# One written order for TensorE in an expert stage, with a split gather, late sums and fewer keep-warm products

## The chip, the cores and the metric

The kernel runs on one NeuronCore of a Trainium2 chip. The metric is the device time of one execution in microseconds. A profile of one execution shows where it goes. Engines are PE (TensorE; PEld is its weight load), DVE (VectorE), ACT (ScalarE), POOL (GpSimd) and SP, which here only issues DMAs.

## The reference

The network is two blocks on 256 tokens of width 1024, all in float32. The first is attention (eight differential half-heads and eight block-attention heads) followed by a mixture of 32 experts; the second is a state-space layer, a stick-breaking attention and two gated embeddings. The change touches the experts. What they compute, with `t` the normed tokens:

```
g = argmax(t @ router_group); top two of the group's eight experts, weights p_group * softmax(top two)
for each expert e and each token sent to it:
    hid = silu(t @ w_gate[e]) * (t @ w_up[e])        # 1024 -> 256
    y[token] += weight * (hid @ w_down[e])           # 256 -> 1024
x = x + y
```

## The kernel before, in words

**Weights.** Each weight is read once. A `Ring` (L89) loads tiles of 1 MB (128 x 2048 floats) from SP's queue in the order of use into the free slots of several pools. A slot comes free when the reads of its tile are through. The 32 experts are 96 such tiles: eight groups of four experts, and per group eight tiles for gate and up (`k` = 0 to 7) and four for down (two halves of columns `c`, two row blocks `k`). Two more tiles, for the embeddings of the second block, are taken behind the third and the fifth group. The tiles of the state-space layer may go into four of the slots alone.

**A group `g` of four experts.** Each expert has 32 slots for tokens, so a group has 128.
- `dispatch` (DVE) writes `disp[g]`, the one-hot of token against slot. There is one buffer for it.
- `gather`: the inputs of the slots, transposed, are products of `x` with `disp[g]`: eight blocks of 128, in two halves `j`. A half is eight matmuls into the one PSUM bank `gx`. Four operations then move it to the tile `xg` with the gain, by turns on DVE (L928) and ACT (L926).
- `pv`: 32 matmuls (eight tiles, four experts beside each other in the array's columns) into one bank; `slot_scale` gives each slot the factor of its token (`rs`); ACT's silu and a DVE operation make `sl`.
- `combine_T` transposes the weighted one-hot: `cmb` says which slot goes to which token, `sw` is the slot's weight.
- Two transposes of `sl` and a DVE copy (L1015) give `hT`. The down products follow: per half `c` eight matmuls into a bank, which ACT moves to `oe` (L1027), times `sw`.
- Two matmuls of `oe` with `cmb` add the half into `sums_of[t][c]`, which stay in PSUM through all groups. Behind the last group they are added to `x`.

**What sets the order.** A planner puts the operations of each engine into an order ahead of time, from their dependencies, from when it thinks that operands are there, and from the order in the program. `after(late, early)` gives it an extra edge, and `in_turn` (L964) chains products: each behind the one before it. Before the change the pv and down products of all groups are in this chain, and the transposes and the sums of the last group. The gather, `slot_scale`, `combine_T`, the other transposes and sums and the projections `ple_proj` are not: the planner places them where it likes. In the trace they stand between the chained products at changing places.

**Other parts of the stage.** `ple_proj` (behind groups 2 and 4, counted from 0) multiplies half of the embedding's input by one weight tile: four units of two matmuls, each into `gx`, each moved out by ACT (L957). Behind group 1 stands `overflow`, a branch for tokens that have no slot; here it isn't taken, but no product crosses it. `keep_warm` (L299) issues products that nobody reads; `warm(7, j)` puts `TAIL[j]` of them between the products of the last group: `j` = 0 to 3 behind tiles k = 3 to 6 of pv, 4 ahead of the transposes, 5 to 8 behind the four down tiles, 9 at the end.

Of the kernel before, what the change touches and what calls it, by code (L numbers as in the profile page):

```python
# [9 lines left out]
F = mybir.dt.float32  # L10
# [10 lines left out]
P = 128  # L21
# [7 lines left out]
# columns of the small-parameter pack  # L29
# [9 lines left out]
# columns of the constant packs  # L39
# [21 lines left out]
TAIL = (8, 3, 3, 2, 1, 3, 2, 3, 2, 6)  # L61
# [3 lines left out]
def merge(*parts):  # L65
    """Runs generators side by side, each at the pace of its number of steps."""
    live = [[g, n, 0] for g, n in parts]
    while live:
        live.sort(key=lambda a: a[2] / a[1])
        a = live[0]  # L70
        a[2] += 1
        try:
            next(a[0])
        except StopIteration:
            live.remove(a)
# [13 lines left out]
class Ring:  # L89
    """Weight tiles of 1 MB in the order of use, loaded ahead into the free slots of a few pools."""  # L90
# [6 lines left out]
    def add(self, name, pool, slots, bufs=None, once=False):  # L97
        """Slots of a tag of a pool, for use again and again or once."""
# [24 lines left out]
    def issue(self):  # L123
        """All reads of the oldest tile taken are in the program."""
# [7 lines left out]
class Halves:  # L132
    """Two tiles [128, 4, 2, 256] as one of [128, 8, 2, 256]."""
# [11 lines left out]
class Dense:  # L145
    """Splits weight tiles into two parts of twelve bits each, ahead of their products."""
# [55 lines left out]
def tile_network(ctx, tc, A, out, dbg=None):  # L202
# [14 lines left out]
    def mm(o, lhsT, rhs, **kw):  # L217
        """A product, issued behind the earlier ones into the same bank."""
# [32 lines left out]
    # ---------------------------------------------------------------- loads that come first  # L251
# [47 lines left out]
    def keep_warm(n, behind, bank=None):  # L299
        """Products that nobody reads: the tensor engine's clock stays up while it waits for data."""  # L300
# [17 lines left out]
    def row_scale(tok, junk, behind):  # L318
        """1 / root mean square of each token."""
# [41 lines left out]
    def scale_of(t, r, sums, eps=EPS):  # L361
        """1 / root of the sum of the two halves' squares."""
# [8 lines left out]
    def tick():  # L371
        """Half a weight tile has been multiplied: emits what was put off until now."""
# [38 lines left out]
    def trans(dense, xT, evac):  # L411
        """out[512 columns, token], K = 1024, weights standing; evac gets two blocks of 128 columns."""
# [50 lines left out]
    # ================================================================ first block: attention  # L463
# [45 lines left out]
    def products(q, k, blk, both):  # L509
        """The products of two heads, side by side in the upper and the lower half of the array."""  # L510
# [7 lines left out]
    def softmax(pa, b):  # L518
        """Exponentials of the masked scores of one head less their maximum, and 1 / their sums."""
# [16 lines left out]
    def transposed(w):  # L536
        """[128 queries, 384] -> [128 keys, 384]: keys 0.. for all queries, keys 128.. for the later ones."""
# [21 lines left out]
    def forward(b, acc):  # L559
        """The parts of block b of yT, and acc with its queries in their order."""  # L560
# [73 lines left out]
    # bias of a distance, as a Hankel table through DRAM: queries run backwards within their tiles of 128  # L634
# [15 lines left out]
    # -lambda on all partitions  # L650
# [325 lines left out]
    def next_xg(g):  # L976
        """The inputs of the four experts after those of g."""
        if g == 7:
            return xg
# [628 lines left out]
```

## Time and profile before

| | |
|---|---|
| three runs, us | 773.49, 777.23, 777.46 (median 777.23) |
| span of the profiled execution, us | 773.4 (the page has no other time of it) |
| busy: PE, PEld | 734.3 us (95%), 517.3 us (67%) |
| busy: DVE, ACT, POOL | 60%, 49%, 14% |
| DMA | 188.77 MB, mean 244 GB/s |

Busy shares are means over the whole span. A matmul's row in the trace lasts until its modelled end, and the next may start long before that: a matmul of four beside each other has a row of about 0.6 us, and four of them start within a few nanoseconds. So a busy PE isn't a full one, and the distance from start to start is the better measure. In this kernel one float32 matmul leaves two records, so `x8` in a row of the timeline is four matmuls. "idle before <- X" says how long the engine had been without work and what released it. `gx`, `tp`, `pv` and `acc` are PSUM banks; `w` are weight tiles.

### The profile page before, as it was taken

Reading aid. Unit: us, or ns where it says so; the run is one execution under the profiler, and the core shown is the slowest. Engines: PE = TensorE matmul, PEld = TensorE weight load, DVE = VectorE, ACT = ScalarE, POOL = GpSimd, SP = SyncE. Lnnn points to the kernel's source line nnn. Section 1 sums busy time; section 2 is a strip of 40 time slices with the busy share of each in tenths; the row PEclk is TensorE's granted clock in tenths of the full one; section 3 lists DMA queues with packets and bytes.
Section 4 is the critical chain, followed back from the end, with each engine's and each line's share of the span. In section 5 each row is a group of like instructions: output and inputs, shape, how many; then the busy total and the mean of one; then the engine's idle time right before and its main releaser. Section 6 shows DMA issues by size and latency. Waiting matters only on the chain. (4 is left out here: it accounts for less than half of the span.)

```text
span 773.4 us, 11374 instructions
## 1 busy us (share of the span) xinstructions
PE 734.3 (95%) x4386; PEld 517.3 (67%) x4386; DVE 467.0 (60%) x887; ACT 380.1 (49%) x712; POOL 110.2 (14%) x74
## 2 busy tenths in 40 slices
PE   8999999997899998899999989999899999999997
PEld 5777767542534334333999988897688897766686
DVE  5658675411101102104999979899888656888974
ACT  6557654210121111103776848475577645756763
POOL 0302300000000000000022231413300301242100
PEclk9999999999899999999999999999999999999999
DMA  8994767899999999983466445444354455222211
GB/s 334 423 404 147 264 238 264 308 412 422 413 422 418 421 420 420 422 369 108 165 242 227 160 151 194 175 164 163 110 184 163 164 177 205 72 104 100 107 56 55
DMA packets 29878, 188.77 MB, mean 244 GB/s; under 512 B 3215, under 2 KB 5852, under 8 KB 8188
## 3 DMA queue, kind: packets, MB, share of 16 engines
q1 hardware_dynamic: 29164, 186.70, 62.5%
q8 instruction: 36, 0.59, 0.3%
q10 hardware_dynamic: 416, 0.62, 0.3%
q0 software_dynamic: 240, 0.67, 0.2%
q14 instruction: 22, 0.18, 0.1%
HBM read 186.88 MB, written 1.10 MB: 243 GB/s over the span
## 5 line engine op out<-in xcount | busy, mean ns | idle before, releaser
L183 DVE TENSOR_TENSOR wl<-w,wh 128x1024 fp32r<-128x1024 f32 x116 | 150.4, 1301 | 49.8 <-ACT wh L172 49.6
L172 ACT ACTIVATE wh<-w 128x1024 fp32r<-128x1024 f32 x117 | 123.1, 1057 | 100.2 <-PE dn L219 86.0
L219 PE MATMUL dn<-uC,wh 128*128 128x256 f32 x640 | 119.5, 288 | 0.6 <-ACT uC L346 0.3
L219 PEld LDWEIGHTS dn<-uC,wh 128*128 128x128 f32 x640 | 100.5, 193 | 2.5 <-issue 1.6
L219 PE MATMUL dn<-uC,wl 128*128 128x256 f32 x320 | 91.2, 285 | 0.0
L187 POOL TENSOR_TENSOR wl<-w,wh 128x1024 fp32r<-128x1024 f32 x18 | 46.6, 2587 | 146.2 <-DVE wh L176 98.4
L997 PE MATMUL pv<-w,xg 128*32 128x512 f32 x512 | 65.8, 596 | 0.0
L219 PEld LDWEIGHTS dn<-uC,wl 128*128 128x128 f32 x320 | 61.9, 193 | 0.2 <-issue 0.2
L315 POOL TENSOR_TENSOR rs_r<-rs_v,mhalf 128x8 f32<-128x8 f32 (+2 forms) x26 | 42.7, 1643 | 119.7 <-DVE rs_v L313 103.5
L928 DVE TENSOR_SCALAR xg<-gx,idg 128x128 f32<-128x128 f32 x30 | 10.5, 350 | 72.0 <-PE gx L219 54.0
L219 PEld LDWEIGHTS gx<-disp,x 128*128 128x128 f32 x240 | 31.1, 200 | 23.6 <-issue 15.3
L219 PE MATMUL dn<-wh,uk 128*128 128x512 f32 x128 | 44.5, 406 | 0.0
L219 PE MATMUL dn<-wh,yTg 128*128 128x512 f32 x128 | 44.2, 407 | 0.3
L219 PE MATMUL gx<-disp,x 128*128 128x128 f32 x240 | 36.2, 296 | 7.7 <-PEq L845 5.0
L936 DVE COPY rs<-tp 128x1 f32<-128x1 f32 x8 | 1.3, 159 | 68.2 <-PE tp L219 68.2
L997 PEld LDWEIGHTS pv<-w,xg 128*32 128x32 f32 x512 | 16.1, 109 | 37.6 <-issue 34.4
L1021 PE MATMUL tp<-w,hT 128*32 128x512 f32 x256 | 37.3, 627 | 1.3 <-DVE hT L1015 1.3
L219 PE MATMUL acc<-oe,cmb 128*128 128x512 f32 x64 | 31.4, 613 | 6.4 <-ACT oe L1027 6.3
L219 PE MATMUL dn<-wh,u 128*128 128x512 f32 x104 | 36.4, 405 | 0.6 <-ACT wh L172 0.6
L926 ACT ACTIVATE xg<-gx,idg 128x128 f32<-128x128 f32 x30 | 11.0, 367 | 52.4 <-DVE xg L928 52.4
L1005 ACT ACTIVATE sl<-pv,rs 128x256 f32<-128x256 f32 x8 | 3.8, 473 | 65.7 <-PE pv L997 37.8
L1027 ACT ACTIVATE oe<-tp,sw 128x512 f32<-128x512 f32 x16 | 11.0, 686 | 43.9 <-PE tp L1021 43.9
(430 smaller groups left out, 1529.0 us busy)
## 6 DMA issues: line engine op xcount, KB each, us to landing
w<-in_wm SPq DMA_DIRECT2D x96, 1024.0 KB, 14.0
w<-in_m SPq DMA_DIRECT2D x28, 1024.0 KB, 4.7
w<-in_ks SPq DMA_DIRECT2D x16, 1024.0 KB, 4.7
w<-in_wi SPq DMA_DIRECT2D x11, 1024.0 KB, 14.3
w<-in_pg SPq DMA_DIRECT2D x8, 1024.0 KB, 4.7
w<-in_wo SPq DMA_DIRECT2D x4, 1024.0 KB, 15.7
eb<-adram SPq DMA_DIRECT2D x8, 512.0 KB, 4.9
w<-in_so SPq DMA_DIRECT2D x4, 1024.0 KB, 4.8
```

Of the source, the lines that this page charges most:

```text
L172: i = nc.scalar.activation(whf, w, AF.Copy)
L183: i = nc.vector.tensor_tensor(wl.rearrange("p a b -> p (a b)"), w, whf.bitcast(F), op=OP.subtract)
L187: nc.gpsimd.tensor_tensor(wl.rearrange("p a b -> p (a b)"), w, whf.bitcast(F), op=OP.subtract)
L219: i = nc.tensor.matmul(o, lhsT, rhs, **kw)
L315: nc.gpsimd.tensor_tensor(r, v, mhalf.to_broadcast([P, n]), op=OP.pow)
L926: nc.scalar.activation(xg[:, k, :], pg_[:, b * P:(b + 1) * P], AF.Copy, scale=gain_of(5, k))
L928: nc.vector.tensor_scalar(xg[:, k, :], pg_[:, b * P:(b + 1) * P], gain_of(5, k), None, op0=OP.mult)
L936: nc.vector.tensor_copy(rs, pt[:, 0:1])
L997: in_turn(nc.tensor.matmul(pgu[32 * e:32 * e + 32, :], xg[:, k, 32 * e:32 * e + 32], w[:, e * 512:(e + 1) * 512], start=k == 0, stop=k == ...
L1005: nc.scalar.activation(sl, pgu[:, 0:256], AF.Silu, scale=rs)
L1021: in_turn(nc.tensor.matmul(po[32 * e:32 * e + 32, :], hT[:, k, 32 * e:32 * e + 32], w[:, e * 512:(e + 1) * 512], start=k == 0, stop=k == 1 ...
L1027: nc.scalar.activation(oe, po, AF.Copy, scale=sw)
```

## The change

All products of the expert stage are chained with `in_turn`, in the order in which they are written. In a group that has a next group to prepare (`ahead`: all but 1 and 7) the order is now:

1. pv of tiles k = 0, 1; the sums of the second half of the group before (`owed`)
2. pv of k = 2, 3; `slot_scale` and `combine_T`
3. pv of k = 4 to 7; the first half of the next group's gather (into `gx`)
4. the transposes of `sl`; then the second half of the gather, into the same bank once it was moved out
5. the down products of both halves; the sums of the first half; in groups 2 and 4 `ple_proj`

The second `oe` gets its own buffer, `oe1`. It shares one with `sl` and `hT`, which become the halves of one tile `slh`. Group 1 keeps its gather behind the branch, now both halves ahead of pv. Group 7 keeps its order, with `slot_scale` and `combine_T` moved. `TAIL` goes from 33 products to 21. Comments and docstrings are taken out, so line numbers stay nearly the same. The core of the diff:

```diff
-TAIL = (8, 3, 3, 2, 1, 3, 2, 3, 2, 6)
+TAIL = (2, 2, 2, 2, 1, 2, 1, 2, 1, 6)
...
-            nc.tensor.transpose(pt[:, t * P:(t + 1) * P], dw[:, t].rearrange("p e c -> p (e c)"), ident)
+            in_turn(nc.tensor.transpose(pt[:, t * P:(t + 1) * P], dw[:, t].rearrange("p e c -> p (e c)"), ident))
...
-            mm(pt[:, 0:1], disp[g][:, t].rearrange("p e c -> p (e c)"), r2[t], start=t == 0, stop=t == 1)
+            in_turn(mm(pt[:, 0:1], disp[g][:, t].rearrange("p e c -> p (e c)"), r2[t], start=t == 0, stop=t == 1))
...
-                    mm(pp_, pT[i][:, k, t * P:(t + 1) * P], w[:, k, c * 512:(c + 1) * 512], start=k == 0, stop=k == 1)
+                    in_turn(mm(pp_, pT[i][:, k, t * P:(t + 1) * P], w[:, k, c * 512:(c + 1) * 512], start=k == 0,
+                               stop=k == 1))
...
+    def gather_products(g, j):
+        pg_ = ps_gx()
+        for b in range(4):
+            ks = slice((4 * j + b) * P, (4 * j + b + 1) * P)
+            for t in range(2):
+                in_turn(mm(pg_[:, b * P:(b + 1) * P], x[:, t, ks], disp[g][:, t].rearrange("p e c -> p (e c)"),
+                           start=b + t == 0, stop=t == 1, skip_group_check=True))
+        return pg_
+    def gather_out(j, pg_, xg):
+        for b in range(4):
+            k = 4 * j + b
+            if b % 2:
+                nc.scalar.activation(xg[:, k, :], pg_[:, b * P:(b + 1) * P], AF.Copy, scale=gain_of(5, k))
+            else:
+                nc.vector.tensor_scalar(xg[:, k, :], pg_[:, b * P:(b + 1) * P], gain_of(5, k), None, op0=OP.mult)
+    def add_up(g, c, oe, cmb):
+        for t in range(2):
+            in_turn(mm(sums_of[t][c], cmb[:, t, :], oe, start=g == 0, stop=g == 7, skip_group_check=True))
...
+            if k == 1 and owed:
+                add_up(*owed.pop())
+            if k == 3:
+                rs = slot_scale(g)
+                cmb, sw = combine_T(g)
...
-        rs = slot_scale(g)
-        sl = mw.tile([P, 256], F, name="sl", tag="sl", bufs=1)
+        slh = mw.tile([P, 512], F, name="slh", tag="slh", bufs=1)
+        sl, hT = slh[:, 0:256], slh[:, 256:512].rearrange("p (k t) -> p k t", k=2)
...
-        cmb, sw = combine_T(g)
+        ahead = g not in (1, 7)
+        if ahead:
+            disp.append(new_disp())
+            dispatch(g + 1)
+            pg_ = gather_products(g + 1, 0)
         warm(g, 4)
         pt = ps_tp()
         for k in range(2):
-            i = nc.tensor.transpose(pt[:, k * P:(k + 1) * P], sl[:, k * P:(k + 1) * P], ident)
-            if g == 7:
-                in_turn(i)
-        hT = mw.tile([P, 2, P], F, name="hT", tag="hT", bufs=1)
+            in_turn(nc.tensor.transpose(pt[:, k * P:(k + 1) * P], sl[:, k * P:(k + 1) * P], ident))
         nc.vector.tensor_copy(hT, pt[:, 0:SEQ].rearrange("p (k t) -> p k t", k=2))
+        if ahead:
+            xg = new_xg()
+            gather_out(0, pg_, xg)
+            pg_ = gather_products(g + 1, 1)
...
+            if c:
+                oe = mw.tile([P, 512], F, name="oe1", tag="slh", bufs=1)
+            else:
+                oe = ra.tile([P, 512], F, name="oe", tag="oe", bufs=1)
             nc.scalar.activation(oe, po, AF.Copy, scale=sw)
...
+            outs.append(oe)
+            if g == 7:
+                add_up(g, c, oe, cmb)
+            elif c == 0 and ahead:
+                gather_out(1, pg_, xg)
+        if g == 7:
+            warm(g, 9)
+            continue
+        add_up(g, 0, outs[0], cmb)
+        if ahead:
+            owed.append((g, 1, outs[1], cmb))
+            if g == 2:
+                ple_proj(0)
+                load_pT(1)
+            if g == 4:
+                ple_proj(1)
+            continue
+        add_up(g, 1, outs[1], cmb)
...
+        for j in range(2):
+            gather_out(j, gather_products(g + 1, j), xg)
```

## Rows read from the trace of the kernel before

**Rows 1.** Windows: stretch, us; busy (x) PE, PEld, DVE, ACT, POOL; PEclk, DMA share, GB/s.
```profile
200.72:342.70 141.98, 131.51 (x828) 54.40 (x828) 21.27 (x65) 21.99 (x46) 0.54 (x1) 1.00 1.01 420
342.70:362.44 19.74, 18.52 (x104) 6.17 (x103) 3.21 (x9) 4.24 (x8) 0.00 (x0) 1.00 0.38 140
362.44:773.00 410.56, 397.10 (x2469) 332.73 (x2468) 339.31 (x509) 262.30 (x459) 86.03 (x50) 1.00 0.42 149
```

**Rows 2.** DMA issues in 322.5 to 323.5 us: count, KB each, us to landing.
```profile
w<-in_wm SPq DMA_DIRECT2D x1, 1024.0 KB, 20.0
```

**Rows 3.** Timeline, 318 to 372 us, PE (start us, us, engine, line, operation, xcount).
```profile
337.85 3.43 PE L303 MATMUL gx<-mhalf 128*1 128x256 f32 x15
...
348.24 0.60 PE L303 MATMUL gx<-mhalf 128*1 128x256 f32 x2
...
358.25 0.63 PE L1021 MATMUL tp<-w,hT 128*32 128x512 f32 x3
```

**Rows 4.** Timeline, 311 to 338 us, PE: a group from pv to pv.
```profile
312.11 7.07 PE L997 MATMUL pv<-w,xg 128*32 128x512 f32 x64
320.39 0.41 PE L1011 MATMUL tp<-idg,sl 128*128 128x128 f32 x2 [1.20 <-DVE sl L1006]
320.96 0.94 PE L219 MATMUL gx<-disp,x 128*128 128x128 f32 x6 [0.16 <-ACT xg L926]
...
326.41 1.98 PE L219 MATMUL acc<-oe,cmb 128*128 128x512 f32 x4 [1.21 <-ACT oe L1027]
328.32 1.06 PE L1021 MATMUL tp<-w,hT 128*32 128x512 f32 x8
329.32 0.61 PE L219 MATMUL tp<-r,disp 128*128 128x1 f32 x4
330.18 0.44 PE L903 MATMUL tp<-idg,dw 128*128 128x128 f32 x2 [0.25 <-DVE rs L936]
330.54 1.07 PE L1021 MATMUL tp<-w,hT 128*32 128x512 f32 x8
...
334.39 3.64 PE L997 MATMUL pv<-w,xg 128*32 128x512 f32 x32
```

**Rows 5.** Timeline, 199 to 216 us, PE: behind the branch.
```profile
202.56 2.05 PE L219 MATMUL gx<-disp,x 128*128 128x128 f32 x16
204.54 6.21 PE L997 MATMUL pv<-w,xg 128*32 128x512 f32 x54
210.68 1.38 PE L219 MATMUL gx<-disp,x 128*128 128x128 f32 x10
```

**Rows 6.** Timeline, 318.2 to 326.5 us, DVE and ACT: reads of gx, then hT.
```profile
319.33 0.35 DVE L928 TENSOR_SCALAR xg<-gx,idg 128x128 f32<-128x128 f32 x1 [6.35 <-PE pv L997]
319.71 0.37 ACT L926 ACTIVATE xg<-gx,idg 128x128 f32<-128x128 f32 x1
...
320.16 0.34 DVE L928 TENSOR_SCALAR xg<-gx,idg 128x128 f32<-128x128 f32 x1
...
320.54 0.37 ACT L926 ACTIVATE xg<-gx,idg 128x128 f32<-128x128 f32 x1 [0.46 <-DVE xg L928]
320.84 0.42 DVE L1015 COPY hT<-tp 128x256 f32<-128x256 f32 x1 [0.34 <-PE tp L1011]
```

**Rows 7.** Timeline, 275.9 to 283 us: two units of a projection half.
```profile
278.94 1.98 PE L219 MATMUL gx<-w,pT 128*128 128x512 f32 x4
280.85 1.06 PE L997 MATMUL pv<-w,xg 128*32 128x512 f32 x8
280.96 0.60 ACT L957 ACTIVATE pp<-gx 128x512 f32<-128x512 f32 x1 [2.31 <-PE gx L219]
```

**Rows 8.** Windows: a stretch of the second group.
```profile
179.90:183.30 3.40, 3.16 (x16) 0.77 (x17) 0.51 (x2) 0.00 (x0) 0.00 (x0) 0.50 1.02 424
```

**Rows 9.** Timeline, 172 to 206 us, PE: the second group behind pv.
```profile
179.18 0.44 PE L1011 MATMUL tp<-idg,sl 128*128 128x128 f32 x2 [1.00 <-DVE sl L1006]
180.14 4.32 PE L1021 MATMUL tp<-w,hT 128*32 128x512 f32 x18 [0.52 <-DVE hT L1015]
```

More of the change, by code (lines that the diff above doesn't have):

```diff
@@ L878, in overflow @@
                         pg_ = pgs[t]
-                        sl = mw.tile([P, 256], F, name="osl", tag="sl", bufs=1)
+                        slh = mw.tile([P, 512], F, name="oslh", tag="slh", bufs=1)
+                        sl, hT = slh[:, 0:256], slh[:, 256:512].rearrange("p (k t) -> p k t", k=2)
                         nc.scalar.activation(sl, pg_[:, 0:256], AF.Silu)
@@ L884, in overflow @@
                             nc.tensor.transpose(pt[:, k * P:(k + 1) * P], sl[:, k * P:(k + 1) * P], ident)
-                        hT = mw.tile([P, 2, P], F, name="ohT", tag="hT", bufs=1)
                         nc.scalar.activation(hT, pt[:, 0:SEQ].rearrange("p (k t) -> p k t", k=2), AF.Copy)
@@ L974, in warm @@
             latest["experts"] = keep_warm(TAIL[j], latest["experts"].ins.name, ps_gx())
-    def next_xg(g):
-        if g == 7:
-            return xg
-        disp.append(new_disp())
-        dispatch(g + 1)
-        t = new_xg()
-        for j in range(2):
-            gather(g + 1, j, t)
-        return t
+    def gather_products(g, j):
[17 more added lines that the diff above has]
+            if g == 7:
+                added.append(add_into_x(t, c, sums_of[t][c]))
+                squares(t, c, xg[:, 0:4, :].rearrange("p a b -> p (a b)"), sums)
     sums = new_sums()
+    added, owed = [], []
     xg = new_xg()
@@ L1000, in tile_network @@
             ring.issue()
+            if k == 1 and owed:
[3 more added lines that the diff above has]
+                cmb, sw = combine_T(g)
             if 2 < k < 7:
                 warm(g, k - 3)
-        rs = slot_scale(g)
-        sl = mw.tile([P, 256], F, name="sl", tag="sl", bufs=1)
+        slh = mw.tile([P, 512], F, name="slh", tag="slh", bufs=1)
+        sl, hT = slh[:, 0:256], slh[:, 256:512].rearrange("p (k t) -> p k t", k=2)
         nc.scalar.activation(sl, pgu[:, 0:256], AF.Silu, scale=rs)
         nc.vector.scalar_tensor_tensor(sl, pgu[:, 256:512], rs, sl, op0=OP.mult, op1=OP.mult)
-        cmb, sw = combine_T(g)
+        ahead = g not in (1, 7)
[3 more added lines that the diff above has]
+            pg_ = gather_products(g + 1, 0)
         warm(g, 4)
@@ L1010, in tile_network @@
         for k in range(2):
-            i = nc.tensor.transpose(pt[:, k * P:(k + 1) * P], sl[:, k * P:(k + 1) * P], ident)
-            if g == 7:
-                in_turn(i)
-        hT = mw.tile([P, 2, P], F, name="hT", tag="hT", bufs=1)
+            in_turn(nc.tensor.transpose(pt[:, k * P:(k + 1) * P], sl[:, k * P:(k + 1) * P], ident))
         nc.vector.tensor_copy(hT, pt[:, 0:SEQ].rearrange("p (k t) -> p k t", k=2))
+        if ahead:
+            xg = new_xg()
+            gather_out(0, pg_, xg)
+            pg_ = gather_products(g + 1, 1)
+        outs = []
         for c in range(2):
@@ L1025, in tile_network @@
                 warm(g, 5 + 2 * c + k)
-            oe = ra.tile([P, 512], F, name="oe", tag="oe", bufs=1)
+            if c:
+                oe = mw.tile([P, 512], F, name="oe1", tag="slh", bufs=1)
+            else:
+                oe = ra.tile([P, 512], F, name="oe", tag="oe", bufs=1)
             nc.scalar.activation(oe, po, AF.Copy, scale=sw)
-            for t in range(2):
-                i = mm(sums_of[t][c], cmb[:, t, :], oe, start=g == 0, stop=g == 7, skip_group_check=True)
-                if g == 7:
-                    in_turn(i)
-                if g == 7:
-                    added = add_into_x(t, c, sums_of[t][c])
-                    squares(t, c, xg[:, 0:4, :].rearrange("p a b -> p (a b)"), sums)
-            if c:
-                warm(g, 9)
-            if g != 1 and c == 0:
-                xg = next_xg(g)
-        if g == 1:
-            latest.clear()
-            overflow()
-            latest.clear()
-            ring.add("xo", ra, 1)
-            ring.add("xt", ra, 1)
-            xg = next_xg(g)
-        if g == 2:
-            ple_proj(0)
-            load_pT(1)
-        if g == 4:
-            ple_proj(1)
+            outs.append(oe)
[3 more added lines that the diff above has]
+                gather_out(1, pg_, xg)
+        if g == 7:
+            warm(g, 9)
[10 more added lines that the diff above has]
+        add_up(g, 1, outs[1], cmb)
+        latest.clear()
+        overflow()
+        latest.clear()
+        ring.add("xo", ra, 1)
+        ring.add("xt", ra, 1)
+        disp.append(new_disp())
+        dispatch(g + 1)
+        xg = new_xg()
+        for j in range(2):
+            gather_out(j, gather_products(g + 1, j), xg)
     phB.close()
@@ L1074, in tile_network @@
         summed = scale_of(t, rC[t], sums)
-    dense.pieces = [added, summed]
+    dense.pieces = [added[-1], summed]
     dense.refill()
```

## The prediction, made before the kernel was run

> **What bounds the kernel now.** The page comes first: TensorE is 95% busy over the span, but that is a mean over stages with different limits, so the stage of the change is looked at by itself, in the windows [rows 1]. From 200.72 to 342.70 us the DMA engines are full (share 1.01, 420 GB/s) and TensorE looks 93% busy as well (131.51 of 141.98). The reader is to see two candidates: the weight stream, which brings a tile of 1 MB every 2.5 us (1.05 MB by 420 GB/s), twelve tiles or 30 us for four experts; and TensorE. The last expert tile separates them. It is issued between 322.5 and 323.5 us and lands 20.0 us later [rows 2], at about 342.7, just where the DMA share falls to 0.38 [rows 1]. TensorE first reads it at 358.25 [rows 3]: it lies there for 15.6 us. The stream got far ahead during attention and the router, and TensorE has still not caught up when the experts end. So the stage ends by TensorE's order, its waits and its keep-warm products; the stream is a floor 15.6 us lower. Behind the stage TensorE goes on with hardly a pause (397 of 411 us) while the DMA engines have a share of 0.42 [rows 1], so what the expert stage gains I carry to the end in full.
>
> **What a group of four experts costs TensorE.** I take distances from the start of one row to the start of the next, where nothing waited; a matmul is two records. Four weight tiles are 32 records, 334.39 to 337.85 = 3.46 us [rows 3, 4], 0.865 a tile, twelve tiles 10.4. One half of the sums, 326.41 to 328.32 = 1.91 [rows 4], two 3.8. One half of the gather (16 records), 202.56 to 204.54 = 1.98 [rows 5], two 4.0. Slot scale and the combine's transposes, 329.32 to 330.54 less 0.25 of waiting = 0.97 [rows 4]. The transposes of sl, 320.39 to 320.96 less 0.16 = 0.4 [rows 4]. That is 19.6 us. Before, pv begins at 312.11 and again at 334.39 [rows 4]: 22.3 us, so 2.7 us of waiting in a group without a projection. The largest pieces are 1.20 for sl and 1.21 for oe [rows 4].
>
> **What the change does to it.** The first half of the next gather (1.98) now stands between pv and the transposes of sl; they came 1.2 us after the end of pv, so that wait is covered. It needs the next disp by then. Slot scale and combine, the last readers of the one disp buffer, move behind the fourth weight tile, which leaves DVE four tiles (3.46 us) to write it under; DVE is 15% busy in the stage (21.27 of 141.98) [rows 1]. The sums of the first half come behind the second half's products, those of the second half behind two tiles of the next group: ACT's oe is covered by 1.7 us each time and the waits for it go. The second oe has a buffer of its own for this.
>
> What is late next: the second half of the gather needs the one bank gx, and in the written order it stands ahead of the down products. The bank is read by DVE, ACT, DVE, ACT one behind the other, 319.33 to 320.91 [rows 6], and the next product into it starts at 320.96 [rows 4]: 1.63 us from the first read, to which I add 0.1 from the last product to that read. From the end of the first half that is 1.73, less the transposes 0.4 = 1.33 us in which TensorE stands and nothing may pass. Behind it wait the eight gather matmuls, the down products, and through them all later weight tiles. Bounds: nothing, if the reads began while products were still made (no row shows that); 2.1, if DVE does hT first (it starts 0.45 behind the transposes, takes 0.42, and then the 1.63 begin; 2.5 less 0.4). I take 1.33, because in rows 6 DVE takes the reads of gx as they come and hT last. A group then takes 20.9 us.
>
> The Trainium skill (PSUM — Partial Sum Buffer, section Terms) says that no two of TensorE, ScalarE and VectorE may touch one bank at once, two reads included. Rows 6 agree: the four reads follow each other although two engines share them. If they could go in pairs the wait would be some 0.8 us shorter, 4 us over five groups; by the rule, and by the rows, it is not.
>
> The two projection halves (ple_proj) are put into the same order. Each is four units of 4 records, 278.94 to 280.85 = 1.91 [rows 7], all into gx. Before, a weight tile ran between two units while ACT emptied the bank. Now the units follow each other and three waits come in: ACT starts at 280.96 and takes 0.60 [rows 7], so the next unit could start at 281.6, 0.75 behind 280.85. A half costs 4 x 1.91 + 3 x 0.75 = 9.9 us. GpSimd's load of the second pT is issued behind it, two groups ahead of its use.
>
> Keep-warm products: 33 become 21. One is two records, 0.43 us (15 records in 3.43 less a tail of 0.2) [rows 3]. Of the twelve taken out eight stood between weight tiles of the last pv (8, 3, 3, 2 becomes 2, 2, 2, 2): 3.4 us of path. Two stood between down tiles: 0.87. Two lay under the wait for oe: nothing.
>
> **The sum.** From the end of the third group's pv (210.68) [rows 5] to the end of the last (348.24) [rows 3] it is 137.6 us. After: five groups 104.5, two projection halves 19.8, eight keep-warm products that remain ahead of the last pv tile 3.4: 127.7, so 9.9 less. With the wait at 2.1 it is 6.0 less, at nothing 16.5, which the stream forbids. The tail behind the last pv: 0.9 less. Ahead of 210.68, in the first group the wait for gx and the covered ones are about equal. In the second, which has no gather beside it, two waits for oe of about 1 us go; but behind the branch of overflow() the gather runs whole ahead of pv, where before its second half lay inside pv (202.56, with pv going on at 204.54 [rows 5]); the time in which gx is emptied then stands open, 1.3 to 1.7 us. I bound this part by 2 less and 1.5 more and take 0.3 less. Together 9.9 + 0.9 + 0.3 = 11.1 us.
>
> The floor: first use of the last tile moves from 358.25 to 347.2, still 4.5 us behind its landing. The DMA queue isn't moved: SP issues a tile when its slot's readers are through, and earlier readers can't make full engines faster.
>
> The profiled execution's span is 773.4 us; the three runs are 773.49, 777.23 and 777.46. 773.4 - 11.1 = 762.3 for that execution, and 777.2 - 11.1 = 766.1 against the median, which is what I predict.
>
> **Rivals.** (A) The waits for gx are at their upper bound, because the order of DVE, which is fixed ahead of time, puts hT, disp or sl ahead of the reads. For it: at 319 to 321 sl and hT stand close to the reads. Against: in rows 6 the reads still come early. In each of six groups 0.8 more is 4.8: 771, at worst 774 if disp is late as well. (B) The waits nearly vanish and the stream bounds the stage: 777.2 - 15.6 = 761.6. For it the full DMA engines, against it the single bank. (C) The change doesn't shorten the groups: the order of before already fills most gaps with whatever is ready, a strict order loses that, and only the keep-warm products are gained: 4.3 less or nothing, 773 to 777. For it 93% busy in the stage; against it the 2.7 us a group above. (D) The other side: the granted clock. In the second group TensorE had 1.00 us idle, two transposes, 0.52 us idle [rows 9], and then stood at half, 1.2 GHz, from 179.9 to 183.3 [rows 8]: 3.4 us at half pace, 1.7 us lost by a fall. An idle piece of 1.3 beside transposes is what six groups now have, three pieces of 0.75 come in each projection half, and the last group has fewer products that fill. With seven falls the gain is gone (11.9); with two a group and one in each projection half the fourteen cost 23.8 us, 12.7 more than the gain: 790. Against it: around 320.39 TensorE had 1.20 and 0.16 us idle about the same transposes [rows 4], and the granted clock of the whole stretch is 1.00 [rows 1].
>
> The Trainium skill (TensorE: Matmul & The Clock Gate, section A second HAM failure mode: psum-queue depth-cycling) speaks for D: small idle pieces between groups of matmuls that cycle through PSUM can make the clock swing. This trace does not agree so far: in 142 us from 200.72, with waits of 1.2 us as in rows 4, the granted clock is 1.00.
>
> **Chances.** Forecast 0.55 (763 to 769.5), A 0.19, B 0.06, C 0.11, D 0.09. A difference under 0.5% (3.9 us) can't be told here from none. Faster by more: the forecast, B and nearly all of A less what of the forecast may be off, 0.76. Within: the rest of A, most of C, a little of D, 0.15. Slower: most of D and the end of C, 0.09. The range: from B at 761.6, less 1.6 because the runs of before spread over 4 us, 760; at the top it takes in A and the first part of C, 774.5.
>
> **What would show it.** Between the weight tiles of a group the sums behind the second and slot scale behind the fourth; 16 gather records behind pv and then the transposes without a wait for sl; one idle piece of 1.3 us that ends with ACT's last read of gx, 16 more gather records, and the down products (an idle piece of 2.1 with hT ahead of a read is A). Three idle pieces of 0.75 in each projection half. The last tile lands at about 342.7 as before and is first read near 347; within 1 us of its landing is B. A group without a projection that takes over 22 us is C. A granted clock under 1.00 between 205 and 345 is D. The prediction falls with any of these, or if the stages behind the experts change by over 2 us.

## The result, and the profile after

| | before | after |
|---|---|---|
| runs on one chip, us | 773.49, 773.61, 777.23, 777.46 (median 775.42) | 763.39, 764.30, 764.38, 765.23 (median 764.34) |
| span of the profiled execution, us | 773.4 | 763.6 (its run: 765.23) |
| first pv of the stage to the end of the sums, us | 146.65 to 362.44 | 148.23 to 351.26 |

The ratio is 0.9853, with a 95% interval of 0.9822 to 0.9884: faster by 11.1 us at the medians. The forecast was 766.1 in a range of 760.0 to 774.5, from 777.2 less 11.1; the kernel before, with one more run, has its median at 775.4, and the same sum from there gives 764.3.

That the sum is met to a tenth is partly luck. The two profiled spans differ by 9.8 us, and that is made of a stage that is 12.8 shorter (215.8 to 203.0), a start of the stage that is 1.6 later, and a rest behind it that is 1.4 longer. The windows of after, with the columns of [rows 1], show the stretches that answer to those and two at half the clock:

```profile
201.35:345.60 144.25, 131.34 (x869) 54.56 (x868) 22.50 (x68) 23.28 (x47) 0.54 (x1) 1.00 1.01 420
345.60:351.26 5.66, 5.26 (x27) 1.63 (x26) 1.70 (x7) 3.08 (x6) 0.00 (x0) 1.00 0.88 352
351.26:763.00 411.74, 398.49 (x2469) 333.83 (x2468) 339.41 (x509) 262.49 (x459) 86.03 (x50) 0.99 0.42 149
139.80:143.20 3.40, 3.40 (x12) 1.50 (x12) 2.39 (x13) 0.48 (x2) 0.58 (x1) 0.50 1.03 361
440.20:446.90 6.70, 6.37 (x30) 6.37 (x31) 4.06 (x6) 2.28 (x4) 0.98 (x2) 0.50 0.66 229
```

Of the 19.7 us that TensorE needed behind the landing of the last expert tile [rows 1], 5.7 are left. The DMA engines are as full as before up to there. The two last rows go with what went against the gain: in the router, ahead of the stage, and in the state-space layer TensorE ran 3.4 and 6.8 us at 1.2 GHz. The same window of before, 139.8 to 143.2, has the clock at 1.00, and before's fall in the state-space layer lasted 3.4. Neither place is touched by the change. The last section shows, from all profiles, that such falls cost about what is missing here.

A group of after, from pv to pv, on TensorE (columns as in [rows 4]):

```profile
313.44 2.05 PE L219 MATMUL gx<-disp,x 128*128 128x128 f32 x16
315.33 0.38 PE L1037 MATMUL tp<-idg,slh 128*128 128x128 f32 x2
317.13 2.05 PE L219 MATMUL gx<-disp,x 128*128 128x128 f32 x16 [1.41 <-ACT xg L991]
319.11 3.64 PE L1049 MATMUL tp<-w,slh 128*32 128x512 f32 x32
322.68 1.98 PE L219 MATMUL acc<-oe,cmb 128*128 128x512 f32 x4
324.59 1.92 PE L1014 MATMUL pv<-w,xg 128*32 128x512 f32 x16
326.45 1.98 PE L219 MATMUL acc<-oe,cmb 128*128 128x512 f32 x4
328.36 1.92 PE L1014 MATMUL pv<-w,xg 128*32 128x512 f32 x16
330.21 0.61 PE L219 MATMUL tp<-r,disp 128*128 128x1 f32 x4
330.68 0.41 PE L903 MATMUL tp<-idg,dw 128*128 128x128 f32 x2
```

This is the written order, and one idle piece is left where [rows 4] had four: 1.41 us, ended by ACT. The 1.20 for `sl`, the 0.25 for `rs` and the 1.21 for `oe` are gone. The same moment on DVE and ACT, answering to [rows 6]:

```profile
315.53 0.35 DVE L993 TENSOR_SCALAR xg<-gx,idg 128x128 f32<-128x128 f32 x1 [0.91 <-PE gx L219]
315.80 0.42 DVE L1038 COPY slh<-tp 128x256 f32<-128x256 f32 x1
315.92 0.37 ACT L991 ACTIVATE xg<-gx,idg 128x128 f32<-128x128 f32 x1 [1.81 <-DVE xg L993]
316.32 0.35 DVE L993 TENSOR_SCALAR xg<-gx,idg 128x128 f32<-128x128 f32 x1
316.71 0.37 ACT L991 ACTIVATE xg<-gx,idg 128x128 f32<-128x128 f32 x1 [0.42 <-DVE xg L993]
```

The four reads of the bank `gx` go one behind the other, 315.53 to 317.08. The copy of `hT` comes behind DVE's first read and lies beside ACT's, so it delays none. The projection units, answering to [rows 7], show the three waits that were foreseen, 0.69 each:

```profile
272.46 1.88 PE L219 MATMUL gx<-w,pT 128*128 128x512 f32 x4
275.03 1.98 PE L219 MATMUL gx<-w,pT 128*128 128x512 f32 x4 [0.69 <-ACT pp L958]
...
280.37 1.98 PE L219 MATMUL gx<-w,pT 128*128 128x512 f32 x4 [0.69 <-ACT pp L958]
282.28 1.07 PE L1014 MATMUL pv<-w,xg 128*32 128x512 f32 x8
```

At the end, the issue of the last expert tile in the window 325.5 to 326 (answering to [rows 2]), and then TensorE's first read of it:

```profile
w<-in_wm SPq DMA_DIRECT2D x1, 1024.0 KB, 19.8
```

```profile
347.07 0.63 PE L1049 MATMUL tp<-w,slh 128*32 128x512 f32 x3
```

It was issued at 325.77 and landed at 345.6, 1.5 us ahead of its use; in before it lay there for 15.6 [rows 2, 3]. The stage has nearly reached its floor.

### The profile page after: what moved, and what is told of

Its sections match the earlier page's. It is cut to its first block, busy times and chain, and to the rows that moved or that the text cites. A ratio compares the mean times of both kernels' runs of the same rounds, so it can differ in the third digit from the quotient of the medians.

```text
span 763.6 us, 11310 instructions
## 1 busy us (share of the span) xinstructions
PE 722.6 (95%) x4362; PEld 515.5 (68%) x4362; DVE 467.2 (61%) x887; ACT 380.9 (50%) x712; POOL 110.2 (14%) x74
## 5 line engine op out<-in xcount | busy, mean ns | idle before, releaser
L183 DVE TENSOR_TENSOR wl<-w,wh 128x1024 fp32r<-128x1024 f32 x116 | 150.5, 1301 | 50.0 <-ACT wh L172 49.9
L1014 PE MATMUL pv<-w,xg 128*32 128x512 f32 x512 | 61.9, 597 | 0.0
L219 PE MATMUL gx<-disp,x 128*128 128x128 f32 x240 | 33.4, 296 | 14.0 <-ACT xg L991 9.1
L1027 ACT ACTIVATE slh<-pv,rs 128x256 f32<-128x256 f32 x8 | 3.8, 474 | 76.4 <-PE pv L1014 76.4
L1049 PE MATMUL tp<-w,slh 128*32 128x512 f32 x256 | 30.5, 596 | 1.0 <-DVE slh L1038 1.0
L1189 DVE SCALAR_TENSOR_TENSOR cv<-raw,cwh,cv 128x256 f32<-128x256 f32 x72 | 30.2, 479 | 1.0 <-ACT cv L1186 1.0
```

What stands on the lines that cost most here:

```text
L183: i = nc.vector.tensor_tensor(wl.rearrange("p a b -> p (a b)"), w, whf.bitcast(F), op=OP.subtract)
L219: i = nc.tensor.matmul(o, lhsT, rhs, **kw)
L1014: in_turn(nc.tensor.matmul(pgu[32 * e:32 * e + 32, :], xg[:, k, 32 * e:32 * e + 32], w[:, e * 512:(e + 1) * 512], start=k == 0, stop=k == ...
L1027: nc.scalar.activation(sl, pgu[:, 0:256], AF.Silu, scale=rs)
L1049: in_turn(nc.tensor.matmul(po[32 * e:32 * e + 32, :], hT[:, k, 32 * e:32 * e + 32], w[:, e * 512:(e + 1) * 512], start=k == 0, stop=k == 1 ...
L1189: nc.vector.scalar_tensor_tensor(v[:, f, :], raw[:, f, j:j + SEQ], cwh[:, 4 * b + j:4 * b + j + 1], v[:, f, :], op0=OP.mult, op1=OP.add)
```

## The experiments

They were timed in three sets, each in five rounds beside the kernel before on one chip. Before's medians there were 775.88 (experiments 1, 2, 6 and 8), 775.70 (3, 4, 7 and 9) and 775.61 (5, 10, 11 and 12), so a comparison across sets is also one across chips, which differ by 0.3 us for the same kernel. The ratios are to before on the same chip. A "period" is the time from the end of one group's pv to the end of the next; "stage" is from the first pv to the last sums in the one profiled execution. "After" in the comparisons is its repetition, the first experiment.

**1. The change again** (no edit).

> The changed kernel once more, as the base for the runs beside it. Both theories: 764.3 us give or take 2, ratio to the kernel before 0.985.

Measured: 763.78 (762.77 to 765.10), ratio 0.9848 (0.9822 to 0.9874). Periods without a projection 21.15, with one 30.9, the last group's 24.58; stage 201.9. The last tile lands at 343.78 and is first read at 344.40. The stage starts at 146.65 here as in before, and the router's window that was at half the clock above is not:

```profile
139.80:143.20 3.40, 3.40 (x19) 1.56 (x19) 2.66 (x14) 0.48 (x2) 0.58 (x1) 1.00 1.00 402
```

So the 1.6 us ahead of the stage were no effect of the change: the same kernel has them in one execution and not in another.

**2. Keep-warm products as before, the rest of the change kept.**

```diff
-TAIL = (2, 2, 2, 2, 1, 2, 1, 2, 1, 6)
+TAIL = (8, 3, 3, 2, 1, 3, 2, 3, 2, 6)
```

> The changed kernel with the 33 keep-warm products of before. Theory (the stage ends by TensorE's own work): ten of the twelve products lie on the path, 0.43 us each, so 4.3 us slower than the changed kernel, about 768.6, and the first use of the last tile moves about 4.3 us further behind its landing. Rival (the weight stream is the bound in the last group, and products only fill the time until a tile lands): under 1.5 us slower, about 765. Second rival (the products held the clock up, and it now falls in places): faster than the changed kernel.

Measured: 769.58 (765.38 to 771.25), ratio 0.9906 (0.9874 to 0.9939), 5.8 above after. In the profile the last group's period is 28.07, 3.49 more, and what follows it 14.54 instead of 13.67, 0.87 more. That is 4.36, the predicted term. The other 1.4 of the medians isn't in the last group, and where it comes from isn't shown. (In this profile the clock fell for 6.8 us at 139.8 and for 10.2 at 194.5, where that of after has 0 and 3.4.)

**3. The other way round: the kernel before with fewer keep-warm products, nothing else.**

```diff
-TAIL = (8, 3, 3, 2, 1, 3, 2, 3, 2, 6)
+TAIL = (2, 2, 2, 2, 1, 2, 1, 2, 1, 6)
```

> The kernel before with the 21 keep-warm products alone. Theory: ten products off the path, 4.3 us less than before, ratio 0.9945, 771.5 where before is 775.8. Rival (the clock falls with fewer products, or they only filled waits): no change, 775 or more, with a granted clock under 1.00 in the last group.

Measured: 770.45 (767.52 to 775.37), ratio 0.9934 (0.9902 to 0.9966), 5.25 below before. The last group's period goes from 29.22 to 25.73: the same 3.49. The order of the other groups is that of before (periods 22.6 and 23.9). From both sides the products are worth 4.4 us in the rows and 5.3 to 5.8 at the medians.

**4. The first half of the gather behind the transposes too.**

```diff
             dispatch(g + 1)
-            pg_ = gather_products(g + 1, 0)
         warm(g, 4)
...
             xg = new_xg()
+            pg_ = gather_products(g + 1, 0)
             gather_out(0, pg_, xg)
```

> Both halves of the gather behind the transposes of sl, the rest as changed. Theory (the first half ahead of the transposes covers sl, and TensorE's order sets the end): in a group sl's wait of 1.25 us comes back, the transposes no longer cover the start of the emptying of gx (0.35), the rest is the same: 1.5 us in each of six groups, 9 us slower than the changed kernel, 773; the rows show an idle piece of 1.2 ahead of the transposes and one of 1.7 between the gather's halves. Rival (the stream is the bound, order only moves slack): under 2 us slower, 766.

Measured: 772.40 (769.61 to 773.30), ratio 0.9954 (0.9937 to 0.9972), 8.6 above after. TensorE in a group:

```profile
259.38 3.64 PE L1014 MATMUL pv<-w,xg 128*32 128x512 f32 x32
264.18 0.44 PE L1036 MATMUL tp<-idg,slh 128*128 128x128 f32 x2 [1.16 <-DVE slh L1028]
264.45 1.95 PE L219 MATMUL gx<-disp,x 128*128 128x128 f32 x16
268.04 2.05 PE L219 MATMUL gx<-disp,x 128*128 128x128 f32 x16 [1.63 <-ACT xg L991]
```

The wait for `sl` that [rows 4] had at 1.20 is back at 1.16, and the one for `gx`, with no transposes under it, is the full 1.63 of [rows 6]. Together the two are 1.38 more than after's one wait of 1.41; the period is 22.56, 1.41 more. So the first half of the gather does what the step said: it covers `sl`, and the transposes then cover a part of the emptying of `gx`.

**5. Slot scale and combine behind all eight pv tiles.**

```diff
-            if k == 3:
-                rs = slot_scale(g)
-                cmb, sw = combine_T(g)
             if 2 < k < 7:
                 warm(g, k - 3)
+        rs = slot_scale(g)
+        cmb, sw = combine_T(g)
```

> The changed kernel with slot scale and combine behind all eight pv tiles instead of the fourth, still in the chain. Theory (they must be early because they hold the one disp buffer): dispatch and with it the first half of the gather wait for them, 0.5 to 0.9 us of idle in each of six groups, 3 to 5 us slower than the changed kernel, 767 to 769. Rival (their place is free): 763.8.

Measured: 770.59 (767.37 to 774.11), ratio 0.9935 (0.9911 to 0.9959), 6.8 above after; more was lost than expected.

```profile
241.01 0.61 PE L219 MATMUL tp<-r,disp 128*128 128x1 f32 x4
...
242.16 0.46 PE L219 MATMUL gx<-disp,x 128*128 128x128 f32 x2 [0.27 <-DVE disp L798]
243.33 1.83 PE L219 MATMUL gx<-disp,x 128*128 128x128 f32 x14 [0.71 <-DVE disp L798]
```

With the readers of the one `disp` buffer so late, DVE writes it while TensorE stands: 0.98 a group in these two waits, and the period is 22.30, 1.15 more. In after's group DVE has four pv tiles for it, and no gather product waits for `disp`. Whether this price and that of the fourth experiment add up wasn't tried.

**6. The sums no longer put off.**

```diff
-            owed.append((g, 1, outs[1], cmb))
+            add_up(g, 1, outs[1], cmb)
```

> The sums of the second half right behind those of the first, not put off into the next group. Theory of the prediction (putting them off takes the wait for oe away, about 1 us in a group): 6 us slower, 770. Rival: the sums of the first half (1.9 us) cover ACT's 0.69 us for the second oe already, and putting off brings nothing: 764, the same.

Measured: 761.95 (760.24 to 763.05), ratio 0.9824 (0.9799 to 0.9849), 1.8 below after. The period is 20.82, 0.33 less, in every group of this kind.

```profile
243.57 3.64 PE L1049 MATMUL tp<-w,slh 128*32 128x512 f32 x32
247.14 3.70 PE L219 MATMUL acc<-oe,cmb 128*128 128x512 f32 x8
250.77 3.64 PE L1014 MATMUL pv<-w,xg 128*32 128x512 f32 x32
```

The second half's sums stand right behind the first half's and wait for nothing: those alone cover ACT's `oe`. And what isn't cut up is shorter from start to start: eight records of sums 3.63 here, 1.91 + 1.91 in after's group (322.68 to 324.59, 326.45 to 328.36); the first 32 of pv 3.57 here, 1.86 + 1.85 there. Together that is 0.33, the whole of the difference. So this part of the change costs about 0.3 us a group and gains nothing.

**7. The new order of the program, but the chain only where it was before.** `in_turn` is taken off `slot_scale`, `combine_T`, the gather, the projections, and the sums and transposes of all groups but the last:

```diff
-            in_turn(mm(sums_of[t][c], cmb[:, t, :], oe, start=g == 0, stop=g == 7, skip_group_check=True))
+            i = mm(sums_of[t][c], cmb[:, t, :], oe, start=g == 0, stop=g == 7, skip_group_check=True)
+            if g == 7:
+                in_turn(i)
```

> The new program order and split, but only the products that were chained before are in the chain; the planner places the rest. Theory (what counts is the order that comes out, not the chain as such): the planner keeps the new order up to the fifth group, puts pv tiles between the projection's units there (2 us shorter in each half) and goes back to sums right behind their down tiles in the last two groups with their waits (about 2 us each): 763 to 766. Rival (the written chain is the gain): back to before apart from the keep-warm products, 769 to 771.

Measured: 765.49 (761.75 to 771.72), ratio 0.9894 (0.9860 to 0.9928). The periods are 29.64, 21.27, 31.75, 23.12, 24.98, against 30.94, 21.15, 30.89, 21.15, 24.58 of after: sum 130.8 against 128.7. Left free, the planner comes close to after in the second of these periods. In the first it lays other products between the projection units, and 29.64 is better than after's 30.94; in the other one with a projection, 31.75, that doesn't come out. It does worst in the period before the last, where two waits for `oe` and one for `rs` are back:

```profile
295.07 1.98 PE L219 MATMUL acc<-oe,cmb 128*128 128x512 f32 x4 [0.81 <-ACT oe L1061]
...
298.84 0.44 PE L903 MATMUL tp<-idg,dw 128*128 128x128 f32 x2 [0.25 <-DVE rs L936]
...
302.67 1.98 PE L219 MATMUL acc<-oe,cmb 128*128 128x512 f32 x4 [0.39 <-ACT oe L1061]
```

In the same period the wait for `sl`, 1.17, stands in place of after's 1.41 for `gx`. Most of what the order gains is there without the chain; the chain is worth 2.0 us in these five periods, 1.2 over the stage (203.1 against 201.9). The spread of these runs (10 us) is too wide to tell 1.7 us between two medians.

**8. The second half of the gather behind the first two down tiles.**

```diff
             gather_out(0, pg_, xg)
-            pg_ = gather_products(g + 1, 1)
...
                 warm(g, 5 + 2 * c + k)
+            if c == 0 and ahead:
+                pg_ = gather_products(g + 1, 1)
```

> The second half of the gather behind the first two down tiles, so that they cover the emptying of gx. Theory (TensorE's waits are the price): the wait of 1.39 us in each of six groups shrinks to the wait for hT, about 0.55, so 0.85 x 6 = 5 us shorter, 759. Rival (the weight stream is now a floor close by: the last tile landed at 345.6 us and was first read at 347.1, 1.5 us later): at most 1.5 to 2 us shorter, 762.5 to 764, with TensorE waiting for tiles in the last group.

Measured: 760.22 (759.45 to 765.00), ratio 0.9809 (0.9778 to 0.9841), 3.6 below after, between the two theories. The last whole group and the end of the stage:

```profile
310.07 0.38 PE L1037 MATMUL tp<-idg,slh 128*128 128x128 f32 x2
311.01 1.93 PE L1048 MATMUL tp<-w,slh 128*32 128x512 f32 x16 [0.56 <-DVE slh L1038]
312.86 2.05 PE L219 MATMUL gx<-disp,x 128*128 128x128 f32 x16
...
328.17 1.07 PE L1014 MATMUL pv<-w,xg 128*32 128x512 f32 x8 [0.36 <-DMA w<-in_wm]
...
330.66 1.06 PE L1014 MATMUL pv<-w,xg 128*32 128x512 f32 x8 [0.57 <-DMA w<-in_wm]
...
333.14 1.06 PE L1014 MATMUL pv<-w,xg 128*32 128x512 f32 x8 [0.57 <-DMA w<-in_wm]
...
343.89 1.06 PE L1048 MATMUL tp<-w,slh 128*32 128x512 f32 x8
```

The wait for `gx` is gone; a shorter one for `hT`, 0.56, takes its place; periods are 20.44, 0.71 less. The four periods between the third group's pv and the seventh's are together 2.9 shorter. The first is 0.3 longer (its wait for `gx` was only 0.36), and the last group gives 1.4 back (25.95 against 24.58): TensorE now stands before weight tiles. The last tile lands at 343.85 and is read at 343.89. The stage is only 0.9 shorter than after's. Most of the rest of the 2.5 us between the two profiles lies behind the stage (406.5 against 408.1), where the clock fell for 3.4 us here and for 6.8 there.

**9. The eighth experiment without the last two expert tiles:** the last group's second down half uses the tiles of its first.

```diff
-MOE_END = 16 + 96 + 2
+MOE_END = 16 + 94 + 2
...
-    moe = [A["wm"][i] for i in range(96)]
+    moe = [A["wm"][i] for i in range(94)]
...
-                w = ring.take()
+                w = kept[k] if g == 7 and c else ring.take()
+                kept.append(w)
...
-                ring.issue()
+                if g < 7 or c:
+                    ring.issue()
```

> The kernel with the second half of the gather behind two down tiles, and the last two expert tiles not loaded: the second half of columns of the last group uses the first half's weights again, so its output differs. Theory (stream as the floor: in that kernel the last tile was read 0.04 us after it landed and the last group took 25.95 us between ends of pv where its work is 23.9): two tiles less of the stream have no effect ahead of the last group's pv, but its second down half no longer waits for a landing: the stage 1 to 3 us shorter, 757.5 to 759. Rival (TensorE's own order is the bound and the floor was coincidence): the same 760.2 give or take 0.7.

Measured: 760.10 (759.61 to 761.56), ratio 0.9804 (0.9778 to 0.9830): no change, so the expectation failed. The edit was badly placed. TensorE's waits for tiles (0.40, 0.57 and 0.57 at the last pv tiles, the period 26.57) stand ahead of the tiles that were left out, and nothing in the ring comes sooner for leaving out what is behind it.

**10. The same with two tiles of the group before the last** (tiles 82 and 83, `g == 6` in the edit).

> The kernel with the second half of the gather behind two down tiles; two expert tiles fewer, this time in the group before the last, whose second down half uses the first half's weights again (its output differs). In the kernel before with two tiles fewer at the very end the waits of the last group stood ahead of those tiles (0.5 to 0.75 us behind each of four keep-warm pairs), so that it told nothing. Theory (the weight stream is the floor): every tile of the last group lands 5 us earlier, the waits between its pv tiles go, 25.95 becomes 23.9 us between ends of pv, and the stage is 2.1 to 2.3 us shorter: 758. Rival (those waits come from TensorE's own order or from ACT and DVE): the same waits, 760.2.

Measured: 761.29 (760.92 to 765.43), ratio 0.9817 (0.9783 to 0.9851). The waits for tiles are gone:

```profile
331.08 0.81 PE L303 MATMUL gx<-mhalf 128*1 128x256 f32 x3
331.52 0.63 PE L1014 MATMUL pv<-w,xg 128*32 128x512 f32 x3
...
336.70 0.63 PE L1014 MATMUL pv<-w,xg 128*32 128x512 f32 x3
```

The last period is 23.86, as expected, and the last tile has landed (341.64) 5.5 us ahead of its use (347.13). So the stream was what held the last group, and from the end of the third pv to the end of the sums it is 138.2 us, against 140.6 in the eighth: the gain that was expected. But the time of the whole kernel isn't lower, against the expectation. The profiled execution was the slowest of the six: it had the clock down for 6.8 us at 140.2, 10.2 at 194.8 and 6.8 at 440.5, and its stage began at 150.70. That alone doesn't explain it: two of the other runs have the mean clock of one of the eighth, 0.989, and its time too, 760.92 and 761.00 against 760.79. Where the 2.4 us go in the whole time stays open.

**11. Eighth and sixth together.**

> Second half of the gather behind two down tiles and the sums not put off: each alone makes a group shorter (0.71 and 0.33 us). Theory (the stream is the floor): 20.1 us a group, but the last group waits longer for its tiles, and from the first pv to the last sums it is 200.9 us as with the late half alone, 760 give or take 0.7. Rival (TensorE's order still sets the end): the shorter groups add up, 6 x 0.33 = 2 us less, 758.

Measured: 760.78 (758.90 to 762.08), ratio 0.9803 (0.9772 to 0.9834): nothing beyond the eighth, although the periods are again 0.34 shorter (20.10). In this profile the end of the third pv is 1.6 us later than in the eighth (208.65 against 207.05), where the clock fell for 10.2 us behind the branch and not for 3.4, and the last group is 0.2 longer (26.17). The last tile lands at 343.50 and is read 0.2 us later, so the stage could hardly have ended sooner:

```profile
343.69 0.63 PE L1048 MATMUL tp<-w,slh 128*32 128x512 f32 x3
```

**12. The eighth without any keep-warm product between the last group's.**

```diff
-TAIL = (2, 2, 2, 2, 1, 2, 1, 2, 1, 6)
+TAIL = (0, 0, 0, 0, 0, 0, 0, 0, 0, 6)
```

> Late half of the gather and no keep-warm products between the products of the last group (the six at the end stay). Theory: TensorE waits for the stream there, so what is left out only becomes idle time, and if the granted clock holds the time is the same, 760. Rival (the products hold the clock): with 0.9 us of work in each 2.5 us of the stream the granted clock falls to half in the last group, a sum half takes 3.8 in place of 1.9 us and so on: 2 to 4 us slower, 762 to 764, with rows under 1.00 between 322 and 352.

Measured: 760.99 (760.14 to 761.91), ratio 0.9802 (0.9771 to 0.9833), the same as the eighth. TensorE in the last group, and the window over it:

```profile
332.29 1.07 PE L1014 MATMUL pv<-w,xg 128*32 128x512 f32 x8 [0.25 <-DMA w<-in_wm]
334.69 1.07 PE L1014 MATMUL pv<-w,xg 128*32 128x512 f32 x8 [1.33 <-DMA w<-in_wm]
336.92 0.44 PE L1037 MATMUL tp<-idg,slh 128*128 128x128 f32 x2 [1.17 <-DVE slh L1028]
```

```profile
327.00:348.40 21.40, 15.66 (x98) 4.01 (x96) 4.12 (x12) 4.36 (x8) 0.00 (x0) 1.00 1.01 421
```

The time that the products took is now idle, partly before tiles and partly before DVE and ACT. The stage ends with the stream all the same: the last tile lands at 344.60 and its sums are through 3.8 us later, as in the eighth. And the clock stayed at 2.4 GHz with TensorE busy for 15.66 of 21.40 us. In the eighth, the eleventh and this one the last tile is read 0.04 to 0.2 us after its landing; as long as it lands then, no order of TensorE's products ends these stages sooner. The three kernels with the late half, at 760.2 to 761.0, are faster than before and after (17 of their 18 runs lie below the lowest of after's ten, 762.77); their intervals don't tell them apart.

## Why the prediction was right, and where it was off

- **What bounds the stage** was right: TensorE's order, its waits and its keep-warm products. From the third group's pv to the last's it was 128.6 us (209.30 to 337.93); the forecast said 127.7.
- **The group**: 20.9 was forecast, 21.15 came. The wait for `gx` was 1.33 by forecast and is 1.41. The twelve weight tiles take 10.84 (3.57 twice, 1.85 twice) and not 10.4: with a change to another kind of product behind them they take about 0.1 us more than the four in [rows 3, 4], behind which keep-warm products came. Slot scale and combine at 0.81 instead of 0.97, and the gather at 3.87 instead of 4.0, give most of that back. The rows show ACT's read of `gx` released by DVE's `xg` ([rows 6] and after's), so the order of the four reads is the program's; what two reads at once would do no run shows. Four such periods make 1.0, the last group 0.3 more; the projection half, 9.9 by forecast, is 9.75 (30.9 less 21.15) and gives 0.3 back.
- **Keep-warm products**: 3.4 and 0.87 by forecast, 3.49 and 0.87 in the second experiment's rows. The tail behind the last pv is 13.33 us instead of before's 14.2.
- **Ahead of the third pv's end**: 0.3 by forecast, bounds 2 less and 1.5 more; it is 3.0 (64.0 to 61.1). This is the term that was mis-sized. 1.6 of it is the fall of the clock at 179.9 [rows 8], which I took for a part of the second group and which is in none of the other profiles. The third experiment has before's order there, and the same 18 records that take 4.32 us in [rows 9] take 2.76 in it (first row below). The rest, 1.4, is inside the bounds, and its parts came as forecast but for one. Up to the second group's transposes before and after take the same 32.53 us. From there to the end of the group's sums after is 2.2 shorter beside the fall (two waits for `oe` of about 1 by forecast). The gather ahead of pv costs 1.4 (1.3 to 1.7 by forecast). The wait at the branch, which the forecast didn't have, is 0.7 shorter: the other two rows, of before and of after, are the first products behind it.

```profile
182.01 2.76 PE L1021 MATMUL tp<-w,hT 128*32 128x512 f32 x18 [0.52 <-DVE hT L1015]
...
196.13 3.75 PE L219 MATMUL gx<-disp,x 128*128 128x128 f32 x16 [4.98 <-PEq L845]
...
193.31 2.77 PE L219 MATMUL gx<-disp,x 128*128 128x128 f32 x16 [4.32 <-PEq L845]
```

- **Sums put off**: a right total with a wrong reason. I wrote that each `oe` is covered by 1.7 us of other products because the sums move away, and priced the move as part of the 2.7 us a group. The waits do go, but the sixth experiment shows that the first half's sums cover the second `oe` by themselves; putting them off costs 0.33 a group.
- **The floor**: I held it at 342.7, 4.5 us ahead of the last tile's use. The use came where it was forecast (347.07 for 347.2), but the tile landed at 345.6, and in the repetition the slack is 0.6 (343.78 and 344.40). By the sign that I had set, under 1 us, that is rival B's picture, though its mechanism isn't there: the waits for `gx` stand at 1.41. Two things were off. The whole stage may start later, and the landing goes with it; and even for the same start (146.5 to 146.7 in seven of the profiles) the last tile landed between 342.66 and 343.85, for a reason that isn't shown. That earlier readers can't make full engines faster was right, and the eighth, eleventh and twelfth experiments ran into just that.
- **Rival A** (waits at the upper bound) is refuted by the row of `hT` at 315.80, behind the first read. **C** (groups not shorter) is refuted by 21.15, where 22 was the bound. **D** (the clock falls) is refuted in the stretch that it was about: 1.00 from 201.35 to 351.26, with an idle piece of 1.4 beside the transposes of each group that prepares a next one. The Trainium skill (TensorE: Matmul & The Clock Gate, section A second HAM failure mode: psum-queue depth-cycling) tells of a kernel in which small idle pieces between PSUM groups made the clock swing; no run here shows it in these groups, not even the fourth experiment with 1.16 and 1.63 in each.
- **The carry to the end** was right but for the clock: 406.4 us behind the first state-space product in before, 407.9 after, 404.9 to 408.1 in the experiments, sorted by how long the clock fell there (last section).

Where the 11 us came from: the keep-warm products are 4.4 in the rows, and the order is the rest, some 6.7. Within the order the split gather and the early slot scale are each needed: 8.6 and 6.8 us are lost without them, each as much as the whole order gains, so these losses are no shares of it. The chain adds 1 to 2, and the sums that are put off less than nothing. That the sums of the first half stand behind the second half's products was not taken out by itself; the seventh experiment alone has two waits for `oe` back (0.81 and 0.39).

## What to carry to other kernels

Price an order by what stands under each wait: put independent products between a product and its consumer where an engine is known to need 1 to 2 us, and let the last readers of a single buffer come early. Ask of every piece that is moved whether what stays already covers the wait; moving more only cuts work up. And when the path comes down to within a few us of the stream, take the floor from several executions and not from one, since further savings in the order end up as waits for tiles.

## What the runs showed of the hardware

The granted clock falls to half at the same three places in most of these profiles, for a time that differs from one execution to another; at the first and the last of them all kernels have the same instructions. (Ten profiles have one more fall at the very end, behind TensorE's last product.) Around 140 us, in the router, the clock was down for 0 us in eight of the fourteen profiles, 3.4 in four, 6.8 in two. Behind the branch, at 190 to 195, it was 3.4 (five), 6.8 (four), 10.2 (four) or 13.7 (one); in the state-space layer, between 437 and 453, 0 (two), 3.4 (seven) or 6.8 (five). In the router's window TensorE was at work without a gap in both cases, and started 12 records at half the clock and 19 at the full one. In the router and in the state-space layer about half of such a fall is lost. The stage starts at 146.5 to 147.0 us in the eight profiles without a fall in the router, at 148.2 to 148.5 in the four with 3.4, and at 150.5 and 150.7 in the two with 6.8. Behind the first state-space product it is 404.9 us in the two profiles without a fall there, 405.8 to 406.7 in the seven with 3.4, and 407.1 to 408.1 in the five with 6.8, whichever kernel it is. Behind the branch, where TensorE stands still for a part of it, a fall costs less: the period over it is 28.69, 29.78 and 30.71 with 3.4, 6.8 and 10.2 us in three profiles that have the same order there (the first experiment, after, the second). So these places alone move an execution by several us: the eight runs of the third experiment lie at 767.5 to 768.2 with a mean clock of 0.995, at 772.7 to 773.3 with 0.989, and at 775.4 with 0.983. That is as large as some of the edits measured here, and no edit is shown to cause it. A profile's span has to be compared with these falls beside it. What decides them stays open.

Against that, behind the branch no waits inside the groups and no lack of keep-warm products brought the clock down: it is 1.00 from the end of the branch's fall to the end of the sums in all fourteen profiles. The one fall inside a group is before's at 179.9 [rows 8]; the third experiment has the same two waits ahead of it, 1.00 and 0.52, and no fall.
